# Two arms per expert, a 32-wide chunk for tokens 65 to 96, half-row scatters and branch hints in a mixture-of-experts kernel

## The chip, the cores and the metric

The kernel runs on 1 core of one Trainium2 chip. The metric is the device time of one execution in microseconds (us); the profile is one execution taken by the hardware profiler. TensorE is called PE here, VectorE DVE, ScalarE ACT, GpSimd POOL, and SyncE, whose queue issues the weight loads, SP.

## The reference

One encoder layer for 256 tokens of width 1024: three token mixers, gates, an output projection and a layer norm, and then a mixture of experts with a second layer norm. The mixers are not touched. The part that matters:

```python
logits = t @ router_w + router_b                    # 256 tokens, 32 experts
top_vals, top_idx = lax.top_k(logits, 4)
gates = softmax(top_vals)
# tokens are grouped by expert; for each expert e and its tokens xe:
h = xe @ w_gu[e] + b_gu[e]                          # 1024 -> 2 x 1024
gate, up = h[:, :1024], h[:, 1024:]
gate = minimum(gate, 7.0); up = clip(up, -7.0, 7.0)
y = ((up + 1) * (gate * sigmoid(1.702 * gate))) @ w_dn[e] + b_dn[e]
out[token] += y * gate_of(token, e)
x = layernorm(DN_ALPHA * x + out)
```

How many tokens an expert gets is known only on the chip.

## The kernel before

The first 396 us of the profiled execution are the mixers and the router; from there on the program walks through the 32 experts in order (`for e in range(NE)`), and ends with the second layer norm.

**Weights.** Expert e has 12 tiles of 1 MB: u0 to u7 for the gate-up product (one per 128 rows of the contraction) and u8 to u11 for the down product. `load(e, u)` puts them into a ring of 19 slots in that order, from SP's queue. A slot is free again when the last matmul that reads its tile has run, and tile u7 of the next expert takes the slot of u0 of this one (seven slots are free beyond an expert's twelve); 8 loads are in flight at most.

**Three arms.** The count of tokens is read from memory into registers of PE, ACT and DVE (`count`, L1294), and two compares choose the arm: L1337 (`rv > TINY`, 32) and inside it L1338 (`rv > CAP`, 64).
- `tiny` (up to 32 tokens): four matmuls at a time on four column groups of 32; tile names end in `t` (`pGU16t`, L1183; down product `pY16t`, L1203).
- `light` (33 to 64): pairs of 64 columns; tiles `pGU` (L1139, L1144) and `pY` (L1162).
- `heavy` (65 to 128): 128 columns; it gathers its own tokens (`heavy_gather`, tiles `pgx15h`, `pgt15h`) with a one-hot that `heavy_onehot` makes on DVE for every expert; gate-up `pGU15h` (L1239), down `pY15h` (L1265).

More than 128 tokens are handled ahead of the last expert, under a compare of its own (L1329). In the profiled run 19 experts take `tiny`, 10 `light` and 3 (experts 2, 15, 17) `heavy`.

**Inside an arm** PE's order is written by hand: bias matmul, gate-up over k = 0 to 7, with another expert's work after k = 1 (`fill` gathers or transposes the tokens of the next pair; `flush(prev)` scatters the expert before), the gates (`gate_slots`) after k = 5, the SwiGLU on DVE and ACT (`swiglu`), a second piece of other work, transposes (`pT`), down product. Then `weigh` splits y times gate into a high and a low part `yh` (ACT) and `yl` (DVE).

**The scatter.** `scatter_lhs` makes the 0/1 matrix `sc` that puts rows back to tokens, as two versions (two `is_equal`, L1112): the result rows of the two column halves stand in partitions 0 to 63 and 64 to 127, and each version has zeros for the other half. `flush` then runs 8 matmuls (L1123, L1124), each over 128 rows, and DVE adds the four results to the accumulator (L1126).

Of the kernel before, what the change touches and what calls it, by code (L numbers as in the profile page):

```python
# [18 lines left out]
P = 128  # L19
D = 1024  # L20
S = 256
# [8 lines left out]
TINY = 32  # L30
LIMIT = 7.0
# [109 lines left out]
def _consts():  # L141
# [26 lines left out]
    slot = np.full((P, 6), -5.0)  # L168
    slot[:64, 0] = p[:64] + 1
    slot[64:, 1] = p[:64] + 1  # L170
    slot[:, 2] = p + 1
    slot[:, 3] = p + 1 + P
    slot[:64, 4] = p[:64] % TINY + 1
    slot[64:, 5] = p[:64] % TINY + 1
# [8 lines left out]
def tile_trunk(ctx, tc, xT_d, xn_d, wf_d, vec_d, row_d, rw_d, cst_d, cst2_d, rope_d, ln1_d, ln2_d,  # L183
# [934 lines left out]
    def scatter(c, n, sc, ys, name):  # L1118
        po = sm(f"pos{name}{c}{n}")
        ls = sc[:, c * P:(c + 1) * P]  # L1120
        w = 512 // len(ys)
        for i, (yh, yl) in enumerate(ys):
            T.matmul(po[:, i * w:(i + 1) * w], ls, yh, start=True, stop=False)  # L1123
            T.matmul(po[:, i * w:(i + 1) * w], ls, yl, start=False, stop=True)  # L1124
        dst = acc[:, c, n * 512:(n + 1) * 512]
        V.tensor_add(dst, dst, po)  # L1126

    def flush(prev):
        if prev:
            e, sc, yh, yl = prev  # L1130
            for c in range(2):
                for n in range(2):
                    scatter(c, n, sc[:, n], [(yh, yl)], f"{e}")

    def light(e, oh, xg, bl, wt, prev, cur, fill):
# [18 lines left out]
        scatter_lhs(e, (0, 1), sc, f"{e}")  # L1154
# [11 lines left out]
    def tiny(e, oh, xg, bl, wt, prev, cur, fill):  # L1166


        nm = f"{e}t"
# [10 lines left out]
        lo = (e % 2) * CAP  # L1180
        for k in range(KT):
            for g, (h, q) in enumerate(quarters):
                T.matmul(grp(ps, g).rearrange("p (g n) -> p g n", g=2), xg[:, k, lo:lo + TINY],  # L1183
                         quarter(wt[k], h, q), start=False, stop=(k == KT - 1))
            if k == 1:
                fill("t") if e % 2 else flush(prev)
            if k == 5:
                gsl = gate_slots(lambda c: oh[:, c, e % 2, 0:TINY], e, nm)
# [5 lines left out]
        flush(prev) if e % 2 else fill("t")  # L1194
        scatter_lhs(e, (4, 5), sc, nm)
        hT = turned(uv, nm, bank(1, f"pT{nm}", [P, 2, P]))
        for b in range(2):
            for h in range(2):
                g = 2 * h + b
                last_ = (b, h) == (1, 1)  # L1200
                for j in range(2):
                    for n in range(2):
                        T.matmul(grp(pY, 2 * n + j), hT[:, j, g * TINY:(g + 1) * TINY],  # L1203
                                 wt[KT + 2 * b + h][:, j, n * 512:(n + 1) * 512],
                                 start=(j == 1 and (b, h) == (0, 0)), stop=last_)
        weigh(pY, gsl, yh, yl)

    def heavy_onehot(e, part):
        oh = ex.tile([P, 2, P], F32R, tag=("ohx", "sg")[part], name=f"ohx{e}h{part}", bufs=2)
# [292 lines left out]
```

## Time and profile before

| | us |
|---|---|
| median of 3 runs (lowest to highest) | 1447.0 (1443.74 to 1450.92) |
| the profiled execution, its own time | 1446.26 |
| its span, first to last instruction | 1444.4 |
| PE busy | 1139.7 (79%) |
| DVE busy | 622.1 (43%) |
| ACT busy | 322.8 (22%) |
| DMA queue 1 (data), share of 16 engines | 79.6%, 454.33 MB |
| DMA queue 8 (instructions) | 120 packets, 1.97 MB |

The averages mix stages with different limits. The stretch to read is the one from 412 us on, by stretches with their DMA rate, and in it the gaps on PE. An idle time whose releaser is called "issue" is one in which the engine waited for nothing that the profile shows.

### The profile page before, as it was taken

To read this page: it belongs to the slowest core of one execution; us is meant where nothing else is said; L and a number is where in the kernel's file an instruction comes from. 1 tells how busy PE (TensorE), PEld (TensorE's weight loads), DVE (VectorE), ACT (ScalarE), POOL (GpSimd) and SP (SyncE) were. 2 spreads that over 40 slices of the span, in tenths; PEclk is the share of its full clock that TensorE was granted. 3 is DMA by queue.
4 is the path that set the end of the run, shared out by engine and by line. 5 is a ranking of instruction groups with operands and counts; after the bars stand their busy time and mean duration, and the time that the engine had idled before them with its cause. 6 is when DMAs were issued, how large, how long until landed. Compare 5 with 4: busy or idle time off the path is not lost. (4 is left out here: it accounts for less than half of the span.)

```text
span 1444.4 us, 18035 instructions
## 1 busy us (share of the span) xinstructions
PE 1139.7 (79%) x6902; PEld 635.4 (44%) x6902; DVE 622.1 (43%) x1289; ACT 322.8 (22%) x651; POOL 294.1 (20%) x293
## 2 busy tenths in 40 slices
PE   8797696899965998778597859869978678766666
PEld 8686586899722442233132325334322233221223
DVE  5999996876642232224222323313232312232203
ACT  5465463654411111011010101111100101100001
POOL 5999999533120000000000000000000000000000
PEclk9998788999888999899798979979999989999778
DMA  7243333477869689999999999966999999999950
GB/s 248 100 146 117 113 133 108 159 237 271 334 234 415 262 341 413 415 415 413 415 415 416 414 413 409 363 260 262 416 413 415 415 415 415 414 414 416 415 231 29
DMA packets 89524, 456.79 MB, mean 316 GB/s; under 512 B 8304, under 2 KB 8704, under 8 KB 58496
## 3 DMA queue, kind: packets, MB, share of 16 engines
q1 hardware_dynamic: 89344, 454.33, 79.6%
q8 instruction: 120, 1.97, 0.6%
q14 instruction: 60, 0.49, 0.1%
HBM read 453.25 MB, written 1.05 MB: 315 GB/s over the span
## 5 line engine op out<-in xcount | busy, mean ns | idle before, releaser
L1391 POOL TENSOR_TENSOR xn<-xn,lb 128x256 f32<-128x256 f32 x4 | 2.8, 726 | 1027.1 <-DVE xn L1379 1027.1
L1144 PE MATMUL pGU<-ew,xg 128*64 128x512 f32 x640 | 159.4, 649 | 0.7 <-issue 0.7
L1126 DVE TENSOR_TENSOR xn<-xn,pos 128x512 f32<-128x512 f32 x124 | 77.1, 680 | 134.0 <-issue 116.1
L393 POOL TENSOR_TENSOR cbc<-cbc,ups 128x256 f32<-128x256 f32 x120 | 123.4, 1029 | 4.6
L248 DVE TENSOR_TENSOR wl<-raw,wh 128x1024 fp32r<-128x1024 f32 (+1 forms) x72 | 99.9, 1394 | 37.3 <-ACT wh L247 37.1
L247 ACT CAST wh<-raw 128x1024 fp32r<-128x1024 f32 (+1 forms) x89 | 91.0, 1030 | 57.0 <-DMA raw<-in_wf_dram 23.4
L392 POOL TENSOR_TENSOR ups<-ups,vec 128x256 f32<-128x256 f32 x120 | 102.2, 871 | 0.0
L1144 PEld LDWEIGHTS pGU<-ew,xg 128*64 128x64 f32 x640 | 46.7, 149 | 95.9 <-issue 94.2
L1162 PE MATMUL pY<-ew,hT 128*64 128x512 f32 x320 | 75.1, 624 | 0.0
L1139 PE MATMUL pGU<-bgu_t,bl 128*128 128x512 f32 x20 | 10.9, 643 | 75.4 <-issue 74.7
L1081 ACT ACTIVATE sg<-gv 128x256 f32<-128x256 f32 x20 | 8.3, 417 | 224.2 <-DVE gv L1079 224.2
L1123 PE MATMUL pos<-yh,sc 128*128 128x512 f32 x124 | 52.8, 426 | 1.7 <-DVE yl L1116 1.7
L248 POOL TENSOR_TENSOR wl<-raw,wh 128x1024 fp32r<-128x1024 f32 x17 | 42.2, 2488 | 52.1 <-ACT wh L247 40.5
L1124 PE MATMUL pos<-yl,sc 128*128 128x512 f32 x124 | 48.8, 394 | 0.0
L1162 PEld LDWEIGHTS pY<-ew,hT 128*64 128x64 f32 x320 | 23.1, 144 | 45.1 <-issue 44.4
L1116 DVE SCALAR_TENSOR_TENSOR yl<-pY,gsl,yh 128x512 fp32r<-128x512 f32 x10 | 7.5, 750 | 80.4 <-ACT yh L1115 80.4
L1139 PEld LDWEIGHTS pGU<-bgu_t,bl 128*128 128x128 f32 x20 | 4.6, 287 | 82.7 <-issue 82.7
L1123 PEld LDWEIGHTS pos<-yh,sc 128*128 128x128 f32 x124 | 23.3, 188 | 29.0 <-issue 21.9
L403 DVE SCALAR_TENSOR_TENSOR xacc<-xp,vec,xacc 128x256 f32<-128x256 f32 x48 | 35.6, 746 | 0.5
L1105 DVE COPY gsl<-pgs 128x1 f32<-128x1 f32 x10 | 1.6, 158 | 76.8 <-PE pgs L1103 76.8
L291 PE MATMUL px<-xh,wh 128*128 128x256 f32 x96 | 29.9, 312 | 5.9 <-ACT pt L553 4.8
L293 PE MATMUL px<-xh,wl 128*128 128x256 f32 x96 | 28.9, 301 | 0.4 <-DVE wl L248 0.4
(1235 smaller groups left out, 2567.4 us busy)
## 6 DMA issues: line engine op xcount, KB each, us to landing
ew<-in_wgu_dram SPq DMA_DIRECT2D x241, 1024.0 KB, 19.9
ew<-in_wdn_dram SPq DMA_DIRECT2D x124, 1024.0 KB, 19.4
raw<-in_wf_dram SPq DMA_DIRECT2D x87, 512.0 KB, 3.6
ew<-in_wgu_dram SPq DMA_DIRECT2D x30, 512.0 KB, 6.3
ew<-in_wdn_dram SPq DMA_DIRECT2D x8, 512.0 KB, 5.7
xraw<-in_xT_dram SPq DMA_DIRECT2D x4, 256.0 KB, 5.1
xn<-in_xn_dram SPq DMA_DIRECT2D x2, 512.0 KB, 6.7
lnt<-in_ln_dram SPq DMA_DIRECT2D x2, 512.0 KB, 10.1
```

Source lines behind the costliest of these rows:

```text
L247: A.copy(h[:, b], raw[:, b])
L248: (PO if u in LOW_POOL else V).tensor_sub(l[:, b], raw[:, b], h[:, b].bitcast(F32))
L291: T.matmul(ps, wh, mh(k), start=(k == 0), stop=False)
L293: T.matmul(ps, wl, mh(k), start=False, stop=(k == nk - 1))
L392: PO.tensor_tensor(pr, up[:, j:j + S], W("cw31", c * 31 + j).to_broadcast([P, S]), op=ALU.mult)
L393: PO.tensor_add(acc, acc, pr)
L403: V.scalar_tensor_tensor(acc, xp[:, j:j + S], W("cw5", t * 5 + j), acc, op0=ALU.mult, op1=ALU.add)
L1123: T.matmul(po[:, i * w:(i + 1) * w], ls, yh, start=True, stop=False)
L1124: T.matmul(po[:, i * w:(i + 1) * w], ls, yl, start=False, stop=True)
L1126: V.tensor_add(dst, dst, po)
L1144: T.matmul(ps[q][h * 64:(h + 1) * 64].rearrange("p (g n) -> p g n", g=2), xg[:, k, s_], quarter(wt[k], h, q), start=False, stop=(k == KT - 1))
L1162: T.matmul(pY[n * 64:(n + 1) * 64], lhs, wt[KT + 2 * b + h][:, j, n * 512:(n + 1) * 512], start=False, stop=(b == 1 and h == 1 and j == 1))
```

## The change

**Arms.** `small` (up to 32) and `light` (above 32) remain, under one compare with a label, `If(rv <= TINY, label=f"few{e}")`. An expert with more than 64 tokens takes `light` for its first 64 and then, under `If(rv > CAP)` inside the Else, `extra_chunk` for tokens 65 to 96: a one-hot of 32 columns, 32 gather matmuls into `pg15m` (L1219), eight copies, and then the body of `tiny` on the same 12 weight tiles, with `flush(cur)` after k = 1. More than 96 tokens go to the block ahead of the last expert. `heavy_onehot` is no longer made for each expert.

**Scatter.** One `sc` with the rows of both halves; each matmul takes 64 rows (partitions 0 to 63 for the first half of the columns, 64 to 127 for the second), and the two halves go to two banks alternately.

**Hints.** The count of expert e + 1 is loaded before expert e's compare, and each arm of e begins on PE with a hint for the branch `few{e+1}`, whose register is the value of `counts[e + 1] > TINY`.

```diff
-    def scatter_lhs(e, slots, sc, name):
+    def scatter_lhs(e, slot_, sc, name):
...
-        for i, s_ in enumerate(slots):
-            V.tensor_scalar(sc[:, i], pbr, C("slot", s_, s_ + 1), None, op0=ALU.is_equal)
+        V.tensor_scalar(sc, pbr, C("slot", slot_, slot_ + 1), None, op0=ALU.is_equal)
...
+    def scatter(pos, c, sc, ys, start=True):
+        for i, y in enumerate(ys):
+            for n in range(2):
+                r = slice(n * 64, (n + 1) * 64)
+                T.matmul(pos[n], sc[r, c * P:(c + 1) * P], y[r], start=(start and i == 0), stop=(i == 1))
...
+    def extra_chunk(e, bl, wt, cur):
+        nm = f"{e}m"
+        oh = ex.tile([P, 2, TINY], F32R, tag="ohm", name=f"oh{nm}", bufs=1)
+        for c in range(2):
+            V.tensor_scalar(oh[:, c], C("iota_s", 0, TINY), rank[c][:, e:e + 1], -float(CAP),
+                            op0=ALU.subtract, op1=ALU.is_equal)
+        pg = sm(f"pg{nm}", [P, KT, TINY])
+        for k in range(KT):
+            for c in range(2):
+                for i, src in enumerate((nh_, nl_)):
+                    T.matmul(pg[:, k], src[:, c, k * P:(k + 1) * P], oh[:, c],
+                             start=(c == 0 and i == 0), stop=(c == 1 and i == 1))
+        xg = ex.tile([P, KT, TINY], F32, tag="xge", name=f"xg{nm}", bufs=1)
+        for k in range(KT):
+            xcopy(xg[:, k], pg[:, k], k)
+        tiny(nm, e, lambda c: oh[:, c], xg, bl, wt, cur, 2, lambda: flush(cur), lambda: None)
...
+    def hint(e):
+        if e + 1 < NE:
+            tc.mark_branch_hint_location(f"few{e + 1}", hint=counts[e + 1] > TINY, engines=(ENG.PE,))
...
-            with tc.If(count(NE, ALL) > P):
+            with tc.If(count(NE, ALL) > TOP):
...
-        rv = count(e, (ENG.PE, ENG.Activation, ENG.DVE))
-        with tc.If(rv > TINY) as some:
-            with tc.If(rv > CAP) as cond:
-                heavy(e, 0, ohx, wt, prev, cur, fill)
-            with cond.Else():
+        rv = counts.pop(e)
+        if e + 1 < NE:
+            counts[e + 1] = count(e + 1, (ENG.PE, ENG.Activation, ENG.DVE))
+        with tc.If(rv <= TINY, label=f"few{e}") as few:
+            with tc.manual_schedule(engines={mybir.EngineType.PE}):
+                hint(e)
+                small(e, oh, xg, bl, wt, prev, cur, fill)
+        with few.Else():
+            with tc.manual_schedule(engines={mybir.EngineType.PE}):
+                hint(e)
+                light(e, oh, xg, bl, wt, prev, cur, fill)
+            with tc.If(rv > CAP):
                 with tc.manual_schedule(engines={mybir.EngineType.PE}):
-                    light(e, oh, xg, bl, wt, prev, cur, fill)
-        with some.Else():
-            with tc.manual_schedule(engines={mybir.EngineType.PE}):
-                tiny(e, oh, xg, bl, wt, prev, cur, fill)
+                    extra_chunk(e, bl, wt, cur)
```

The first place is PE at expert 15, where the code of `tiny` ends and that of `light` begins. Before:

```order
L1203 MATMUL pY15t<-ew_15_11_11853,hT15t 32x512 x4
L1337 UNCONDITIONAL_BRANCH
L1338 COMPARE_AND_BRANCH
L1139 MATMUL pGU_12083<-bgu_t,bl_11371 128x512
L1139 MATMUL pGU_12084<-bgu_t,bl_11371 128x512
L1144 MATMUL pGU_12083<-ew_15_0_11831,xg_10354 64x512 x2
```

Now, at the same place:

```order
L1197 MATMUL pY15t<-ew_15_11_10959,hT15t 32x512 x4
L1334 UNCONDITIONAL_BRANCH
L1291 REGISTER_ALU
L1495 BRANCH_PREFETCH_HINT
L1136 MATMUL pGU_11099<-bgu_t,bl_10535 128x512
L1136 MATMUL pGU_11100<-bgu_t,bl_10535 128x512
L1141 MATMUL pGU_11099<-ew_15_0_10937,xg_9640 64x512 x2
```

The second compare (L1338) stood between the two arms; it is gone from there, and a register operation and the hint stand in its place.

The second place is PE at the end of `light` of expert 15. Before, the code of `heavy` followed behind a jump:

```order
L1162 MATMUL pY_12144<-ew_15_10_11851,hT_1_12189 64x512 x4
L1162 MATMUL pY_12144<-ew_15_11_11853,hT_1_12189 64x512 x4
L1338 UNCONDITIONAL_BRANCH
L980 MATMUL pgt15h_11867<-cst,rawx 128x128 x4
L980 MATMUL pgt15h_11876<-cst,rawx 128x128 x4
```

Now the compare with 64 follows, and straight behind it the gather of the extra chunk:

```order
L1159 MATMUL pY_11160<-ew_15_10_10957,hT_1_11204 64x512 x4
L1159 MATMUL pY_11160<-ew_15_11_10959,hT_1_11204 64x512 x4
L1342 COMPARE_AND_BRANCH
L1219 MATMUL pg15m<-oh15m,nh 128x32
L1219 MATMUL pg15m<-oh15m,nl 128x32
```

The jump at the end of `light` has become a compare, and the extra chunk begins after the last down product of `light`.

The third place is `flush` in the light arm of expert 15, on PE. Before, each bank gets its two matmuls in a row:

```order
L1123 MATMUL pos_12162<-yh,sc 128x512
L1124 MATMUL pos_12162<-yl,sc 128x512
L1123 MATMUL pos_12166<-yh,sc 128x512
L1124 MATMUL pos_12166<-yl,sc 128x512
L1123 MATMUL pos_12170<-yh,sc 128x512
```

Now two banks take turns:

```order
L1117 MATMUL pos_11178<-yh,sc 128x512
L1117 MATMUL pos_11179<-yh,sc 128x512
L1117 MATMUL pos_11178<-yl,sc 128x512
L1117 MATMUL pos_11179<-yl,sc 128x512
L1117 MATMUL pos_11186<-yh,sc 128x512
```

The number of matmuls stays at eight; neighbours now work on different halves of the rows and write different banks.

## Rows read from the trace of the kernel before

**Rows 1.** Stretches: length; PE, PEld, DVE, ACT, POOL busy (count); PEclk, DMA share, GB/s

```profile
470.00:520.00 50.00, 49.65 (x145) 23.63 (x145) 13.95 (x33) 5.18 (x12) 0.00 (x0) 1.00 0.67 252
...
900.00:920.00 20.00, 20.00 (x75) 9.01 (x73) 6.45 (x17) 3.40 (x8) 0.00 (x0) 1.00 0.80 308
...
950.00:1010.00 60.00, 58.25 (x174) 29.75 (x174) 17.81 (x44) 8.70 (x21) 0.00 (x0) 0.94 0.61 231
1010.00:1370.00 360.00, 270.14 (x1737) 98.69 (x1737) 99.43 (x247) 34.46 (x74) 0.00 (x0) 0.90 1.02 415
```

**Rows 2.** DMA rate in 2-us slices, 440 to 520 us and 940 to 1020 us

```profile
GB/s 422 422 412 410 406 401 412 401 430 418 414 422 410 422 414 422 336 78 66 406 324 254 8 0 0 227 328 328 338 328 418 418 426 320 16 0 176 369 279 426
...
GB/s 426 397 422 414 418 422 418 385 86 0 0 0 33 295 371 344 14 137 387 264 289 352 418 250 49 348 332 311 12 0 33 311 229 414 414 414 430 408 393 412
```

**Rows 3.** SP's queue: what the weight loads waited for, 860 to 1012 us; issues; landing

```profile
SPq L732 <- PE pGU17h L1239: 30.4, 2, 24.4
...
859.66 18.43 SPq L732 DMA_DIRECT2D ew<-in_wgu_dram  x8
...
DMA to landing us min/median/max: 4.7/19.9/21.5
```

**Rows 4.** PE in order of time, arm beginnings: start, us, instructions, idle before and releaser

```profile
461.77 0.76 PE L966 MATMUL pgx2h<-nh,ohx2h 128*128 128x512 f32 x1 [14.99 <-issue]
...
864.46 1.97 PE L980 MATMUL pgt15h<-cst,rawx 128*128 128x128 f32 x8 [16.02 <-issue]
...
951.37 1.97 PE L980 MATMUL pgt17h<-cst,rawx 128*128 128x128 f32 x8 [14.82 <-issue]
...
1107.60 1.93 PE L1178 MATMUL pGU22t<-bgu_t,bl 128*32 128x512 f32 x8 [3.97 <-issue]
```

**Rows 5.** Instruction queue, packets and MB, in three gaps: before a small, light, heavy arm

```profile
q8 instruction: 1, 0.02, 1.1%
...
q8 instruction: 2, 0.03, 1.1%
...
q8 instruction: 3, 0.05, 1.3%
```

**Rows 6.** PE in order of time: end of 14, beginning of 16, light 18 whole

```profile
844.80 3.64 PE L1203 MATMUL pY14t<-ew,hT14t 128*32 128x512 f32 x32 [0.53 <-ACT hT14t L1094]
...
917.67 1.07 PE L1178 MATMUL pGU16t<-bgu_t,bl 128*32 128x512 f32 x8
918.56 1.90 PE L1183 MATMUL pGU16t<-ew,xg 128*32 128x512 f32 x16
...
1005.69 0.70 PE L1139 MATMUL pGU<-bgu_t,bl 128*128 128x512 f32 x2 [0.38 <-PE pos17h L1124]
...
1035.86 1.94 PE L1178 MATMUL pGU19t<-bgu_t,bl 128*32 128x512 f32 x8 [2.54 <-issue]
```

**Rows 7.** PE in order of time, pieces of small 22 and 23, first and last of eight scatters

```profile
1111.91 0.50 PE L1123 MATMUL pos<-yh,sc 128*128 128x512 f32 x1
...
1113.63 0.39 PE L1124 MATMUL pos<-yl,sc 128*128 128x512 f32 x1
...
1136.09 1.09 PE L980 MATMUL pgt23t<-cst,rawx 128*128 128x128 f32 x8
```

**Rows 8.** ACT and DVE in order of time: weighing, the two comparisons for the scatter

```profile
1381.62 0.69 ACT L1115 ACTIVATE yh<-pY,gsl 128x512 fp32r<-128x512 f32 x1 [9.32 <-PE pY L1162]
...
1415.00 0.86 DVE L1112 TENSOR_SCALAR sc<-pbr,cst 128x256 fp32r<-128x256 f32 x2
```

**Rows 9.** PE in order of time, the last two experts (30 and 31), and SP's last issues

```profile
1347.87 1.19 PE L1139 MATMUL pGU<-bgu_t,bl 128*128 128x512 f32 x2 [10.56 <-issue]
...
1397.98 1.19 PE L1139 MATMUL pGU<-bgu_t,bl 128*128 128x512 f32 x2 [12.67 <-issue]
...
1418.26 8.67 PE L1162 MATMUL pY<-ew,hT 128*64 128x512 f32 x32
...
1369.12 22.21 SPq L735 DMA_DIRECT2D ew<-in_wdn_dram  x4
```

More of the change, by code (lines that the diff above doesn't have):

```diff
@@ L30 @@
 TINY = 32
+TOP = CAP + TINY
 LIMIT = 7.0
@@ L1116, in weigh, with add @@
         V.scalar_tensor_tensor(yl, pY, gsl, yh.bitcast(F32), op0=ALU.mult, op1=ALU.subtract)
[L1118 to L1124, printed above, removed]
+    def scatter(pos, c, sc, ys, start=True):
[3 more added lines that the diff above has]
+                T.matmul(pos[n], sc[r, c * P:(c + 1) * P], y[r], start=(start and i == 0), stop=(i == 1))
+    def add(c, n, po):
         dst = acc[:, c, n * 512:(n + 1) * 512]
@@ L1260, in heavy @@
-        pY = [bank(n, f"pY{nm}{n}") for n in range(2)]
-        for n in range(2):
-            T.matmul(pY[n], bls[n], bdn_t, start=True, stop=False)
-        def down(n, b, h, j):
-            T.matmul(pY[n], hT[h, b][:, j], wt[KT + 2 * b + h][:, j, n * 512:(n + 1) * 512],
-                     start=False, stop=(b == 1 and h == 1 and j == 1))
-        for b in range(2):
-            for h in range(2):
-                for j in range(2):
-                    if (b, h) == (1, 1):
-                        continue
-                    for n in range(2):
-                        down(n, b, h, j)
@@ L1275, in heavy @@
[L1275 to L1287 removed]
+        scatter_lhs(e, 3 + part, sc, nm)
@@ new lines, in heavy @@
+        hT = {hq: turned(swiglu(ps[hq], f"{nm}_{hq[0]}{hq[1]}"), f"{nm}_{hq[0]}{hq[1]}") for hq in qs}
+        for n in range(2):
+            pY = bank(n, f"pY{nm}{n}")
+            T.matmul(pY, bls[n], bdn_t, start=True, stop=False)
+            for b in range(2):
+                for h in range(2):
+                    for j in range(2):
+                        T.matmul(pY, hT[h, b][:, j], wt[KT + 2 * b + h][:, j, n * 512:(n + 1) * 512],
+                                 start=False, stop=(b == 1 and h == 1 and j == 1))
+            weigh(pY, gsl, yh, yl)
+            for c in range(2):
+                po = sm(f"pos{nm}{c}{n}")
+                for i, y in enumerate((yh, yl)):
+                    T.matmul(po, sc[:, c * P:(c + 1) * P], y, start=(i == 0), stop=(i == 1))
+                add(c, n, po)
@@ L1359, in total, with add1 @@
                     T.matmul(pz[c][n], C("ident"), acc[:, c, n * 512:(n + 1) * 512], start=True, stop=False)
-            for n in range(2):
-                for i, y in enumerate((yh, yl)):
-                    T.matmul(pz[c][n], sc[:, n, c * P:(c + 1) * P], y, start=(c == 1 and i == 0), stop=(i == 1))
-        def add(n):
+            scatter(pz[c], c, sc, (yh, yl), start=(c == 1))
+        def add1(n):
             dst = acc[:, 1, n * 512:(n + 1) * 512]
```

97 lines of the change are left out of this document (34 added, 63 removed).

## The prediction

> **What bounds the kernel now.** I read the DMA rate by stretches first. From 1010 to 1370 us the queues move 415 GB/s [rows 1], which is their steady level in this kernel; a 1 MB tile then takes 2.53 us and an expert's twelve 30.3 us. So the weights set the pace, and PE's work costs time only where it keeps a ring slot so long that loads stop. The stretches where they stop are those around the three heavy experts: 252, 308 and 231 GB/s [rows 1]. Against 415 GB/s the lost time is 50 x (1 - 252/415) = 19.6 us at expert 2, 20 x (1 - 308/415) = 5.2 us behind expert 15 and 60 x (1 - 231/415) = 26.6 us behind expert 17; together 51.4 us. The view of SP's waits names the cause: loads wait up to 24.4 us for a heavy gate-up matmul [rows 3]. The slices show where the data ran dry: the rate falls at 473.6 us and at 956.4 us (336 and 86 GB/s as shares of a 2-us slice) [rows 2].
>
> Next come the gaps on PE. Its time between two arms is idle with the releaser "issue", and its length goes in steps: 3.97 us from a small arm to a small one [rows 4], 10.6 us from a small arm to a light one [rows 9], 15.0, 16.0 and 14.8 us from a small arm to a heavy one [rows 4]. In such gaps the instruction queue brings 1, 2 and 3 packets [rows 5]. One more compare that doesn't fall through is one more packet and about 5 to 6 us. At the end weights no longer bound: the last four loads are issued from 1369 to 1391 us, and PE stands 12.7 us before expert 31 and then works to the end [rows 9].
>
> **The change part by part.** All times are on the scale of the profiled execution, 1446.3 us, which lies 0.7 us below the median.
>
> *Entry of a heavy expert.* One compare of two goes, so the gap falls from 15.3 (mean of three) to a light arm's; with 10.6 and rows like it between 9.4 and 11.0 I take 10.3. Saved: 5.0 us of PE each.
>
> *Body of a heavy expert.* Before: 864.46 to 917.67, 53.2 us [rows 4, 6]. After: a light visit and the extra chunk. The light visit of expert 18 is 1005.69 to 1035.86 - 2.54 = 27.6 us [rows 6]. It loses one of two comparisons that take 0.86 us together [rows 8], 0.43, and part of the scatter: eight matmuls start 0.24 us apart, 1.9 us in all [rows 7]. That pairs on different halves of the rows run at once isn't shown here, but four column groups do (16 matmuls of a small arm in 1.90 us, 4 x 0.48) [rows 6]. I take half, 0.94, with 0 as the other end. So 27.6 - 1.4 = 26.3 us; experts 15 and 17 do transposes (1.1 us [rows 7]) where 18 does a gather of about 1.9, so 25.5.
>
> The extra chunk, until it has read the first weight tile: it waits for the weighing of the 64 tokens (0.69 on ACT [rows 8] and about as much on DVE) and two one-hots of below 0.43 each: 2.3. Then 32 gather matmuls; the nearest row is eight 128x128 transposes in 1.09, 0.136 each [rows 7]: 4.4. Copies that aren't hidden 0.5, bias 1.07, and the first of eight gate-up steps 0.93 [rows 6]. Sum 9.2 us, with 6 and 12 as ends (gathers twice as fast or as slow, copies in line or hidden). Behind it: seven gate-up steps 6.5, scatter 0.94, bias of the down product about 1.0, SwiGLU and transposes 2.4, down product 3.64 (as in a small arm [rows 6]): 14.5. The chunk is 23.7, the whole visit 50.0 (49.2 for 15 and 17): only 3 to 4 us shorter than before.
>
> *Which slot is late.* This matters more than the visit's length. Before, tiles were freed one by one over the visit. Now none is free until the extra chunk has read it, and then they come free every 0.93 us, faster than 2.53. So the first tile decides. From issue to landing takes at least 4.7 us [rows 3], 2.2 before the bytes flow.
> - Expert 2: the arm before ends at 461.77 - 14.99 = 446.8 [rows 4]. First slot at 446.8 + 10.3 + 26.3 + 9.2 = 492.6, bytes at 494.8; dry since 473.6. Loss 21.2 instead of 19.6: +1.6.
> - Expert 15: the arm before ends at 848.4 [rows 6]; first slot at 848.4 + 10.3 + 25.5 + 9.2 = 893.4, bytes at 895.6. Expert 16's u0 is issued at 859.7, lands 19.9 later, and u6 six tiles on, at 894.7 [rows 3]. Loss 0.9 instead of 5.2: -4.3.
> - Expert 17: expert 15 ends at 848.4 + 10.3 + 49.2 = 907.9; small 16 takes 951.37 - 14.82 - 917.67 = 18.9 [rows 4, 6], less 1.4, so 925.7 with the step between. First slot at 925.7 + 10.3 + 25.5 + 9.2 = 970.7, bytes at 972.9; dry at 956.4 - 4.3 = 952.1. Loss 20.8 instead of 26.6: -5.8.
> Sum of the heavies: -8.5 us. An error of x in the 9.2 counts at 2 once and at 17 twice: 3x.
>
> *Tail.* Expert 31's gap loses the second compare, -5.0; light 30 gets 1.4 shorter and its scatter 0.9; light 31 0.4; the last scatter 0.5, since only its first results are waited for. Sum -8.2 (-5 without the pairs).
>
> *What costs nothing.* Register loads and the hint lengthen each arm by some tenths at most, and a small visit with its gap is 22.9 us against 30.3 of loads; the cover is gone at 15 to 17 and at the end, where they are within the error. The one-hots taken off DVE hid in its idle time. Where small and light arms get shorter between 1010 and 1370 us, loads stay the bound.
>
> *The hint.* Nothing in this trace has one. From below: it does nothing, and gaps stay. From above: the gap before a light arm becomes that before a small one, 10.3 to 4.0. I take the lower end. The arm in which the hint stands goes on for 19 to 28 us and ends in a jump that itself brings a packet [rows 5]. And the register says `counts[e + 1] > TINY` while the branch is written `rv <= TINY`: by the gaps, small is the way that costs nothing, so a hint that speaks of the written condition speaks for the wrong way.
>
> [...]
>
> **Sum:** 1446.3 - 8.5 - 8.2 = 1429.6, say 1430 us. With 3 us either way in the extra chunk (9 us) and the scatter's 0, 1420 to 1441.
>
> **Rivals.**
> *The hint works.* Each heavy gap falls by another 6.3: expert 2 loses 14.9 (-6.3), 15 nothing (-0.9), and 17's first slot comes 12.6 earlier, with dry time 0.9 earlier (-11.7): -18.9. In the tail 30's gap gives 6.3 and 31's about 5, and PE stands less; the cap is the last tile: issued at about 1391, landed by some 8 us later, and read for 2 us, 1402 against PE's 1418.26 + 8.67 = 1426.9 [rows 9], so at most 25 us with the 8.2 in it; I take 24. Total 1446.3 - 8.5 - 18.9 - 24 = 1395 us (1388 to 1405). For it: the hint stands where the gap is made; against it: the two reasons above.
>
> *The hint speaks for the wrong way and throws out the next code.* Then a small arm pays about 5.3 us more. Alone, 22.9 + 5.3 = 28 is still under 30.3; it shows at expert 16, ahead of 17's first slot: +5.3, 1435 us.
>
> *The extra chunk comes later than thought, and the time ends above before.* Its code lies behind `light`'s and has its own compare on PE, ACT and DVE. Each packet that it must wait for is 5.3 us ahead of the first slot, and counts three times, 15.9. Break-even is 16.7 / 3 = 5.6 us per chunk: one packet gives 1446, two give 1462 us, since the twelve slots held are exactly what the loads then lack. For it: no run has executed code at this place, and 2.54 us are lost even behind light 18 [rows 6], where the old `light` jumped past `heavy`. Against: the arm that follows a compare directly costs no packet beyond the jump's own [rows 5].
>
> **How the numbers follow.** Chances: forecast 0.45 (1420 to 1441), hint works 0.31, wrong way 0.09, late chunk 0.15 (about half of it at one packet). The likeliest is 1430. The range runs from 1388 (the good end of the working hint) to 1444, which leaves out about 0.08 below and 0.1 above. 0.5% of 1447 is 7.2 us, about what a measurement of this kernel tells from no change: below 1439.8 lie nearly all of the first two and most of the third, 0.80; 0.11 lie within; 0.09 above.
>
> **What would show it.** Gaps on PE before light arms at 9.4 to 11 us mean that the hint does nothing, 4 or less that it works, and small arms with an inner gap of 5 that it harms. The loads' stop behind expert 2 should be as long as before and that behind 17 shorter by about 6; `pg15m` should follow `pY` by 2 to 3 us, and the first gate-up row of `pGU15m` by another 6. Expert 31's gap should be 7 to 8 us. The prediction is wrong in its core if the loads stop for another tile than the first, or if the end is set by something other than these waits.

## The result: 57 us slower

The changed kernel takes 1502.7 us (median of 4 runs, 1500.9 to 1503.9), the kernel before, run beside it, 1445.4 (1438.1 to 1450.9). The ratio is 1.040 with an interval of 1.035 to 1.045. The forecast was 1430 with a range up to 1444: wrong in sign and out of the range. The profiled execution took 1503.9 us, its span is 1502.0; before 1446.3 and 1444.4.

First the page: busy time of PE, and the instruction queue (packets, MB, share of the DMA engines). Of the kernel before:

```profile
PE 1139.7 (79%) x6902; PEld 635.4 (44%) x6902; DVE 622.1 (43%) x1289; ACT 322.8 (22%) x651; POOL 294.1 (20%) x293
...
q8 instruction: 120, 1.97, 0.6%
```

Of the changed kernel:

```profile
PE 1138.3 (76%) x7322; PEld 602.6 (40%) x7322; DVE 599.7 (40%) x1187; ACT 319.0 (21%) x636; POOL 291.9 (19%) x293
...
q8 instruction: 123, 2.02, 0.5%
```

PE is busy for as long as before, so the 57 us are time in which PE stands. The stretches of the changed kernel, with the columns of [rows 1], say where the loads stood:

```profile
470.00:500.00 30.00, 27.65 (x143) 12.76 (x141) 7.62 (x18) 2.85 (x6) 0.00 (x0) 0.96 0.16 67
500.00:540.00 40.00, 33.97 (x218) 12.52 (x220) 8.47 (x21) 4.79 (x11) 0.00 (x0) 0.86 0.77 316
540.00:560.00 20.00, 16.84 (x100) 5.97 (x100) 8.57 (x20) 2.29 (x5) 0.00 (x0) 1.00 0.29 106
560.00:900.00 340.00, 241.57 (x1481) 85.97 (x1475) 77.98 (x182) 31.72 (x67) 0.00 (x0) 0.86 1.00 405
920.00:945.00 25.00, 23.22 (x156) 11.32 (x153) 4.92 (x12) 2.21 (x5) 0.00 (x0) 0.80 0.60 234
995.00:1030.00 35.00, 31.84 (x204) 13.16 (x202) 10.72 (x26) 3.81 (x9) 0.00 (x0) 0.85 0.37 130
1050.00:1070.00 20.00, 17.55 (x94) 6.72 (x90) 5.07 (x13) 2.86 (x6) 0.00 (x0) 1.00 0.43 169
1070.00:1380.00 310.00, 210.31 (x1400) 71.70 (x1400) 70.56 (x163) 28.08 (x59) 0.00 (x0) 0.86 1.00 407
1430.00:1502.00 72.00, 44.52 (x196) 19.25 (x192) 17.27 (x42) 5.77 (x11) 2.77 (x4) 0.78 0.37 141
```

Reckoned as in the prediction (length times 1 - rate/415), the first two lines are the stop at expert 2: 25.2 + 9.5 = 34.7 us, where [rows 1] had 19.6. The third is a stop that the kernel before did not have, behind light 3: 14.9. Behind expert 15 10.9 are lost instead of 5.2. At 17 and behind light 18 it is 24.0 + 11.9 instead of 26.6. Where the loads ran at 415 before, from 520 to 900 and from 1010 to 1370, they now run at 405 (8.2 lost, from 560 to 900) and at 407 (6.0 lost). From 412 to 470 us they run at 386 instead of 406 (4.1 lost instead of 1.3). Together some 115 us of loading are lost up to 1430 us, where the kernel before lost 53; the difference of 62 is the 57 us to within 5. The end costs nearly what it cost before: 72 x (1 - 141/415) = 47.5 us in the last line, and in the last 74 us of the kernel before, at 139 GB/s, 49.2. So the stops at 2 and 15 grew, new ones came behind light arms, and none got shorter but 17's own.

What the weight loads waited for, in SP's queue from 412 to 1480 us (total, times, longest):

```profile
SPq L727 <- PEq L1342: 164.9, 9, 32.7
...
SPq L727 <- PE pGU2m L1178: 46.7, 3, 45.8
...
SPq L727 <- PE pGU17m L1178: 37.6, 3, 36.7
```

Line 1342 is `with tc.If(rv > CAP)`, the compare of the extra chunk, and PEq is PE's sequencer. Nine times a load waited for that compare, so not for a matmul. Before, a light arm freed its tiles one by one: from 412 to 1400 us the loads waited for a matmul of line 1144, a light arm's gate-up, 9.2 us at the longest.

```profile
SPq L732 <- PE pGU L1144: 36.5, 13, 9.2
```

PE's own waits in the changed kernel, from 412 to 1480 us: the gaps ahead of light arms and then every stop of over 3 us inside an arm:

```profile
PE pGU L1136 <- issue: 107.8, 12, 11.4
PE pGU21t L1178 <- issue: 6.8, 1, 6.8
PE pGU5t L1178 <- issue: 6.7, 1, 6.7
PE pGU23t L1178 <- issue: 6.7, 1, 6.7
...
PE pGU9t L1178 <- issue: 6.2, 1, 6.2
PE pGU27t L1178 <- issue: 6.0, 1, 6.0
...
PE pGU1t L1178 <- issue: 5.6, 1, 5.6
...
PE pGU29t L1178 <- issue: 5.5, 1, 5.5
...
PE pGU13t L1178 <- issue: 4.0, 1, 4.0
...
PE pGU19t L1178 <- issue: 3.9, 1, 3.9
...
PE pGU11t L1178 <- issue: 3.5, 1, 3.5
```

Line 1136 is the first matmul of a light arm (as 1139 in the kernel before), so its 107.8 us are the gaps ahead of lights. Line 1178 is a gate-up matmul in the middle of an arm. Ten small arms stand still there, every one of an odd expert, 54.9 us in all. PE in order of time shows the first of them and what it does to expert 2 (start, length, instructions, idle before and releaser); in the last line small 4, behind light 3, waits 1.78 us for DVE to pass the compare on line 1342:

```profile
427.86 1.93 PE L1174 MATMUL pGU1t<-bgu_t,bl 128*32 128x512 f32 x8 [4.35 <-issue]
429.54 3.66 PE L1178 MATMUL pGU1t<-ew,xg 128*32 128x512 f32 x14
438.81 1.86 PE L1178 MATMUL pGU1t<-ew,xg 128*32 128x512 f32 x2 [5.60 <-issue]
...
465.18 1.19 PE L1136 MATMUL pGU<-bgu_t,bl 128*128 128x512 f32 x2 [9.51 <-issue]
466.30 5.78 PE L1141 MATMUL pGU<-ew,xg 128*64 128x512 f32 x16
472.01 0.50 PE L1117 MATMUL pos<-yh,sc 64*128 64x512 f32 x2
472.35 0.39 PE L1117 MATMUL pos<-yl,sc 64*128 64x512 f32 x2
...
487.36 7.09 PE L1159 MATMUL pY<-ew,hT 128*64 128x512 f32 x32
496.32 0.25 PE L1219 MATMUL pg2m<-oh2m,nh 128*128 128x32 f32 x1 [1.87 <-DVE oh2m L1213]
...
501.77 1.94 PE L1174 MATMUL pGU2m<-bgu_t,bl 128*32 128x512 f32 x8
503.48 2.53 PE L1178 MATMUL pGU2m<-ew,xg2m 128*32 128x512 f32 x16
...
554.90 1.06 PE L1174 MATMUL pGU4t<-bgu_t,bl 128*32 128x512 f32 x8 [1.78 <-DVEq L1342]
```

In the kernel before the same small arm began at 428.71 and the gap ahead of expert 2 at 446.8, so it took 18.1 us. Now it runs from 427.86 to 465.18 - 9.51 = 455.67, which is 27.8. The stop itself is 5.60; the rest is slower matmuls on both sides of it: the changed kernel needs 3.66 us for the 14 gate-up matmuls ahead of the stop where the one before did 16 in 2.52, and behind it the transposes, 1.09 us at a granted clock of 1.00 [rows 7], took 1.97 at 0.50. PE's granted clock is 0.51 from 427 to 433.2 us, behind the gap ahead of the arm. It has risen to 1.00 when the stop begins (433.2 to 436), falls while PE stands and is 0.50 from 436.5 to 442; in the kernel before it is 0.76 from 430.4 to 433 and 1.00 from 434 to 438. PE's records show no branch between 427.5 and 438.8 us, so the stop is not a jump.

### The profile page after: what moved, and what is told of

It reads as the page before. It is cut to its first block, busy times and chain, and to the rows that moved or that the text cites. A ratio compares the mean times of both kernels' runs of the same rounds, so it can differ in the third digit from the quotient of the medians.

```text
span 1502.0 us, 18859 instructions
## 1 busy us (share of the span) xinstructions
PE 1138.3 (76%) x7322; PEld 602.6 (40%) x7322; DVE 599.7 (40%) x1187; ACT 319.0 (21%) x636; POOL 291.9 (19%) x293
## 5 line engine op out<-in xcount | busy, mean ns | idle before, releaser
L1141 PE MATMUL pGU<-ew,xg 128*64 128x512 f32 x832 | 212.1, 659 | 1.1 <-issue 1.1
L1121 DVE TENSOR_TENSOR xn<-xn,pos 128x512 f32<-128x512 f32 x136 | 84.6, 681 | 141.5 <-PE pos L1117 141.5
L388 POOL TENSOR_TENSOR cbc<-cbc,ups 128x256 f32<-128x256 f32 x120 | 121.4, 1012 | 4.6
L1141 PEld LDWEIGHTS pGU<-ew,xg 128*64 128x64 f32 x832 | 64.3, 152 | 127.4 <-issue 123.0
L1136 PE MATMUL pGU<-bgu_t,bl 128*128 128x512 f32 x26 | 15.0, 678 | 107.8 <-issue 107.8
L1159 PE MATMUL pY<-ew,hT 128*64 128x512 f32 x416 | 95.3, 612 | 0.0
L1159 PEld LDWEIGHTS pY<-ew,hT 128*64 128x64 f32 x416 | 29.6, 141 | 56.6 <-issue 55.9
L1117 PE MATMUL pos<-yh,sc 64*128 64x512 f32 x136 | 30.5, 444 | 1.8 <-DVEq L1342 1.8
L287 PE MATMUL px<-xl,wh 128*128 128x256 f32 x96 | 28.7, 299 | 0.0
L1109 ACT ACTIVATE yh<-pY,gsl 128x512 fp32r<-128x512 f32 x13 | 8.9, 687 | 90.2 <-PEq L1342 68.7
```

Of the source, the lines that this page charges most:

```text
L287: T.matmul(ps, wh, ml(k), start=False, stop=False)
L388: PO.tensor_add(acc, acc, pr)
L1117: T.matmul(pos[n], sc[r, c * P:(c + 1) * P], y[r], start=(start and i == 0), stop=(i == 1))
L1141: T.matmul(ps[q][h * 64:(h + 1) * 64].rearrange("p (g n) -> p g n", g=2), xg[:, k, s_], quarter(wt[k], h, q), start=False, stop=(k == KT - 1))
L1159: T.matmul(pY[n * 64:(n + 1) * 64], lhs, wt[KT + 2 * b + h][:, j, n * 512:(n + 1) * 512], start=False, stop=(b == 1 and h == 1 and j == 1))
```

## The experiments

Fifteen kernels were run. Times are medians of four runs or more with the ratio to the kernel before in the same batch (95% interval); one is a single run, and says so. "Small first" means that the small arm's code lies directly behind the expert's compare, as in both kernels.

### The hints

**e1_no_hint**: the changed kernel without the two calls.

```diff
-                hint(e)
                 small(e, oh, xg, bl, wt, prev, cur, fill)
...
-                hint(e)
                 light(e, oh, xg, bl, wt, prev, cur, fill)
```

> The changed kernel without the hints; all else stays. Theory A (the hint's fetch goes ahead of the next block of the running arm, so small arms whose code crosses a block early stand still): the inner gaps of 3.5 to 6.8 us in ten odd small arms (54 us together) go away, visits of odd small arms fall from about 28 to 19 us, and the time falls to 1430 to 1450 us. Theory B (the gaps come from the new layout of the code, the hint does nothing): inner gaps and time stay, 1495 to 1510 us. Theory C (the extra chunk's held tiles are the cost): time falls by under 10 us.

Measured: 1478.7 us, 1.026 (1.023 to 1.029). The hints cost some 20 to 24 us of the 57 (1.4% by the two ratios, 24 us by the medians). In PE's waits only 2.9 us at small 20 and 1.4 at 22 are left for "issue" at line 1178. So theory A was right on the inner gaps, but the time stayed 29 us above its 1430 to 1450: the hints are not the whole loss. Without them expert 2 begins at 453.27 us instead of 465.18, and 26.5 us of loading are lost there (452 to 512 us at 232 GB/s) instead of 34.7.

**e2_flip**: the same calls with the other sign.

```diff
-            tc.mark_branch_hint_location(f"few{e + 1}", hint=counts[e + 1] > TINY, engines=(ENG.PE,))
+            tc.mark_branch_hint_location(f"few{e + 1}", hint=counts[e + 1] <= TINY, engines=(ENG.PE,))
```

> The changed kernel with the hint's condition turned round (count of the next expert <= 32). If the value decides what is fetched: gaps ahead of light arms fall from 9.5 us to 4 or less. If the value doesn't matter: gaps of 9.3 to 11.4 us ahead of light arms, the same ten odd small arms with inner gaps, and 1495 to 1510 us.

Measured: 1460.3 us in a single run, 13 us below the lowest of e1's four. The stops inside small arms fall from 54.9 to 1.7 us (1.4 at expert 5 and 0.3 at 23), with the same instructions at the same places. So it is the sign of the hint that makes them. The gaps ahead of lights stay at 9.5 to 11.5 where a small arm was before: even the other sign does not shorten them, so neither expectation held whole. From light to light, ahead of experts 7 and 25, they are 2.1 and 2.1, where the changed kernel has 7.0 and 7.0 and e1 1.8 and 5.5.

**e4_before_hint**: the kernel before, with the counts read one expert ahead and the hints as the change has them.

```diff
+            tc.mark_branch_hint_location(f"few{e + 1}", hint=counts[e + 1] > TINY, engines=(ENG.PE,))
...
+                    hint(e)
...
+                hint(e)
```

> The kernel before with the hints alone (early counts, label and hint in the small and light arms). Theory A: small arms get inner gaps of 3 to 7 us, 1465 to 1500 us. Theory B (layout): no new gaps, 1440 to 1452 us.

Measured: 1466.1 us, 1.016 (1.013 to 1.019): 23 us slower, with nothing of the change but the hints and the early counts, which this run does not separate. Here other arms are hit (entry of 11 7.4 us instead of none, inside 20 6.7, 27 6.2, 13 5.0), so what is hit changes with the code and does not belong to the expert.

### The block behind light

**e3_three**: no hints, and no block behind light: light, or a second copy of light with the extra chunk in the same arm (edit against e1).

```diff
-            with tc.manual_schedule(engines={mybir.EngineType.PE}):
-                light(e, oh, xg, bl, wt, prev, cur, fill)
-            with tc.If(rv > CAP):
+            with tc.If(rv <= CAP) as one:
                 with tc.manual_schedule(engines={mybir.EngineType.PE}):
+                    light(e, oh, xg, bl, wt, prev, cur, fill)
+            with one.Else():
+                with tc.manual_schedule(engines={mybir.EngineType.PE}):
+                    light(e, oh, xg, bl, wt, prev, cur, fill)
                     extra_chunk(e, bl, wt, cur)
```

> No hints, and three arms: small, light, and a copy of light with the extra chunk behind it, so that light has no compare behind its down product. Theory (light's inner compare makes PE wait for DVE's last step behind each light arm): the 1.78 us waits for DVE ahead of ten arms go away, and the time is 3 to 12 us below that of the run without hints. Rival (those waits are hidden under the loads): within 3 us of it, or above by up to 15 us since a heavy expert pays two compares again.

Measured: 1453.6 us, 1.008 (1.005 to 1.011). Against e1 the block costs 25 us, more than the 3 to 12 expected: the theory was about a wait of 1.78 us for DVE, and what went away is the hold on the tiles. In e1 SP's queue still has the wait that the changed kernel has (line 1340 is there the same compare); in e3 there is none:

```profile
SPq L727 <- PEq L1340: 150.7, 9, 32.2
```

The stop of the loads goes with it. Light 3 begins at 510 us in e1 and at 511 in e3; the stretch from there on, first e1 (14.6 us lost) and then e3 (nothing lost):

```profile
512.00:552.00 40.00, 36.08 (x227) 13.32 (x225) 12.64 (x30) 4.50 (x10) 0.00 (x0) 1.00 0.66 264
```

```profile
512.00:552.00 40.00, 36.16 (x188) 12.39 (x190) 11.14 (x26) 3.93 (x9) 0.00 (x0) 0.90 1.02 414
```

**e5_hold** and **e6_join**: does the block cost because it reads the weights, or because of the join? The kernel before gets an If behind light that is never taken (no count exceeds 200 here). In e5 its body reads all twelve tiles; in e6 it reads the identity instead.

```diff
+                with tc.If(rv > 200):
+                    with tc.manual_schedule(engines={mybir.EngineType.PE}):
+                        pd = sm(f"pd{e}", [P, P])
+                        for u in range(12):
+                            w_ = wt[u] if u < KT else wt[u][:, 0]
+                            T.matmul(pd, w_[:, 0:P], C("ident"), start=(u == 0), stop=(u == 11))
```

and for e6, against e5:

```diff
-                            w_ = wt[u] if u < KT else wt[u][:, 0]
-                            T.matmul(pd, w_[:, 0:P], C("ident"), start=(u == 0), stop=(u == 11))
+                            T.matmul(pd, C("ident"), C("ident"), start=(u == 0), stop=(u == 11))
```

> The kernel before, with one thing added behind light: an If that is never taken here (count over 200) whose body reads all twelve weight tiles of the expert. Theory (a block behind light that may read the tiles holds all twelve slots of every light expert until PE has passed its compare): SP's loads wait for that compare up to 30 us at a time, the data rate falls behind light experts, and the time rises by 10 to 30 us. Rival (only the wait of the engines for each other at the join costs): as the next run.

> The same If behind light, never taken, whose body reads no weight tile. Theory of the held slots: tiles are freed one by one as before, only the join is left, 0 to 8 us above the kernel before. Rival (the join is the cost): as much as the run in which the body reads the tiles.

Measured: e5 1435.0 us, 0.994 (0.991 to 0.997); e6 1418.9, 0.983 (0.980 to 0.986). Reading the tiles in a block that never runs costs 16 us, the difference of the two. In e5 SP waits 20.3 us at the longest for that compare, in e6 2.8 (3.5 us in all):

```profile
SPq L732 <- PEq L1343: 25.3, 2, 20.3
```

But against the kernel before both came out the other way than expected: e5 is 8 us faster instead of 10 to 30 slower, and e6, which only adds work that is never done, is 25 us faster. The reason stood in the gaps, of both runs: in e6 ahead of lights behind small arms -0.1 instead of 9 to 11 us, from light to small 9.3 to 9.7 instead of -0.1. These are the gaps of an order in which small lies last, as the next run has it.

### The order of the arms

**e9_small_last**: the kernel before with one argument more.

```diff
-        with tc.If(rv > TINY) as some:
+        with tc.If(rv > TINY, preferred_fallthrough_block=True) as some:
```

> The kernel before with one word changed: the branch on 32 tokens is laid out with the small arm last, so that a small arm runs on into the next expert's compares and light or heavy follow those without a jump; no block behind light. Theory (which arm lies next to the next compare decides where the gaps fall; the run with the block that reads nothing was faster for that alone): gaps ahead of light and heavy arms behind small ones fall from 9 to 16 us to below 1, gaps ahead of small arms behind light ones rise from 0 to about 9, and the time is 1408 to 1425 us. Rival (the speed of that run came from the join itself): 1440 to 1450 us.

Measured: 1414.3 us, 0.979 (0.976 to 0.982). The instructions of the arms are the same. PE's waits of the kernel before, from 412 to 1400 us, and then those of e9:

```profile
PE pGU L1139 <- issue: 74.7, 8, 12.7
```

```profile
PE pGU L1139 <- issue: 14.7, 3, 9.8
PE pGU13t L1178 <- issue: 11.4, 1, 11.4
...
PE pGU4t L1178 <- issue: 9.7, 1, 9.7
PE pGU8t L1178 <- issue: 9.6, 1, 9.6
```

The gaps ahead of lights fall from 74.7 to 14.7 us, those ahead of heavies from 15 and 16 [rows 4] to 2.5 and below, and light to small rises from about zero to between 9 and 11. The sum of the gaps is not the gain; their place is. A gap ahead of a small arm is covered by the loads, one ahead of a heavy arm is time in which no slot comes free, and one ahead of light 30 or 31 stands at the end of the program. From 412 to 1360 us the loads run at 400 GB/s instead of 392, 948 x 8/415 = 18 us; the gap ahead of light 30 falls from 10.56 [rows 9] to -0.1, that ahead of 31 from 12.67 to 9.8.

**e11_after_small_last**: the changed kernel, hints and block and all, with small last.

```diff
-        with tc.If(rv <= TINY, label=f"few{e}") as few:
+        with tc.If(rv <= TINY, label=f"few{e}", preferred_fallthrough_block=False) as few:
```

> The changed kernel, hints and all, with the small arm laid out last; the hint's register is then set when the branch is not taken. Theory (value 0 speaks for the jump: it now speaks the right way, and the layout saves the gaps ahead of light): no inner gaps in small arms, gaps ahead of light arms behind small ones near 0, the loads still stop behind light arms (held slots): 1435 to 1465 us. Rival (hints cost whatever they say): 1470 us or more.

Measured: 1430.1 us, 0.989 (0.986 to 0.992), 5 us below the range expected. This one argument moves the changed kernel by 73 us, from 4.0% slower to 1.1% faster. It does two things at once, since with the order of the arms it turns what the hint speaks for: here the hints as written help, small to small is -0.2 to 1.9 us instead of 4.2 to 6.0. The block still holds the slots (PEq L1342: 104.7 us in 9 waits, longest 33.0).

### The extra chunk, and putting it together

**e12_extra_last**: e3 (light, light with the chunk, small; no hints) with small last. **e13_interleaved_last**: the same, but the third arm takes each weight tile for the 64 tokens and for the 32 two steps later. **e7_interleaved** is that arm in e3's order. The core of the interleaved arm:

```diff
+        for k in range(KT):
+            mt(k)
+            if k + 2 < KT:
+                lt(k + 2)
```

> The layout of the small-last run (light, then the arm above 64, then small), no hints, no block behind light, half-row scatters; above 64 tokens light and behind it the extra chunk on the held tiles. Beside the small-last run, whose arm above 64 is the old heavy, it shows the chunk alone. Theory (the first slot comes late): loads stop 15 to 22 us at expert 2 and at 17, against 10 and 5, and the time is 10 to 20 us above the small-last run, 1424 to 1434. Rival (the chunk is as good as heavy): within 5 us of it.

> The same layout, with the interleaved arm above 64 tokens lying behind light, so that its exit passes the small arm alone. Theory (the 13.5 us gaps behind the interleaved arm in the earlier run came from a jump over two arms): they fall below 2 us, and the time falls from 1431 to 1400 to 1415 us. Rival (the interleaved arm itself is slow): 1425 us or more.

> Three arms without hints; in the third, tokens 65 to 96 are done together with the first 64: each gate-up tile is read by the extra chunk two steps behind the 64 tokens and then free, and the extra down product follows the first one. If the late first slot was the cost at the heavy experts: loss at expert 2 falls from 23 to about 10 us, at 15 and 17 from 30 to 10 or 15, and the time is 15 to 30 us below the three-arm run, 1425 to 1440. If the length of PE's visit was the cost: within 8 us of it.

Measured: e12 1412.2 us, 0.976 (0.972 to 0.981). It differs from e9 in the form of the heavies (and the scatter in halves) and lies within its interval: two chunks of 64 and 32 are worth as much as the old heavy arm, and the 10 to 20 us expected for a late first slot did not come. Against e3, which has its three arms with small first, e12 shows what the order is worth without hints: 1.008 to 0.976, 3.2%. e13 1403.8, 0.972 (0.968 to 0.976): freeing tiles from the start of the arm gives some 8 us, though the two intervals overlap. e7 1445.9, 1.002 (1.000 to 1.004): in the old order the same gives 8 us against e3 as well, where 15 to 30 were expected, and no more than brings it back to the kernel before.

**e10_best**: the interleaved arm (`wide`), but in the order wide, light, small (edit against e13).

```diff
-            with tc.If(rv <= CAP, preferred_fallthrough_block=True) as one:
+            with tc.If(rv > CAP) as one:
...
-                    light(e, oh, xg, bl, wt, prev, cur, fill)
+                    wide(e, oh, xg, bl, wt, prev, cur, fill)
...
```

> Small arm last, the interleaved arm for tokens 65 to 96 in place of heavy, half-row scatters, no hints, no block behind light. If the two gains add: the gaps of the small-last run and a loss of loads at the heavy experts below it, 1395 to 1415 us. If the interleaved arm gives nothing beside the layout: within 5 us of the small-last run.

Measured: 1431.4 us, 0.989 (0.985 to 0.993), 28 us behind e13 and 16 us above the range expected. Now the wide arm jumps over two others, and what follows it waits 13.5 us (experts 3, 16 and 18). In e13 that gap is 0.8 us at 3 and 6.6 at 18, but still 13.3 at 16, where a small arm follows. And light no longer lies next to the compare: from small to light the gap is 3.9 to 5.8 us, in e13 -0.1.

**e14_hints_right**: e13 with the hints as the change writes them, which in this order are right.

```diff
+                    hint(e)
                     light(e, oh, xg, bl, wt, prev, cur, fill)
...
+                hint(e)
                 small(e, oh, xg, bl, wt, prev, cur, fill)
```

> The run before with the hints as the change writes them, which is the right way round in this layout (0 speaks for the jump to the small arm). If right hints help: gaps from small to small fall from 4 to below 1 us and from light to small below 9, time 0 to 10 us lower. If they cost: inner gaps in small arms and 5 us or more above.

Measured: 1393.1 us, 0.965 (0.962 to 0.969): 51 us faster than the kernel before and 110 faster than the changed one. PE in order of time at the beginning of small 1, e13 and then e14:

```profile
430.62 1.93 PE L1174 MATMUL pGU1t<-bgu_t,bl 128*32 128x512 f32 x8 [4.38 <-issue]
432.30 3.67 PE L1178 MATMUL pGU1t<-ew,xg 128*32 128x512 f32 x16
```

```profile
425.80 1.04 PE L1174 MATMUL pGU1t<-bgu_t,bl 128*32 128x512 f32 x8
426.66 1.90 PE L1178 MATMUL pGU1t<-ew,xg 128*32 128x512 f32 x16
```

The gap is gone, and the matmuls behind it take half the time (1.90 instead of 3.67): the granted clock is 1.00 from 425.9 to 428.5 us in e14, and 0.50 in e13 from 430.6 to 434, behind its gap. PE's sequencer has a record for each branch, and the one ahead of small 1 says where the gap comes from, first e13 and then e14 (length in ns three times, start):

```profile
L1419 PEldq COMPARE_BRANCH  x1: 6532/6532/6532, 423.9 to 423.9; - x1
```

```profile
L1419 PEldq COMPARE_BRANCH  x1: 370/370/370, 423.7 to 423.7; - x1
```

It starts while the last matmuls of small 0 still run; so of the 6.53 us only 4.38 show as a gap. From light to small, where the light arm ends in a jump over two arms, the gap only falls from 9.3 to 7.8 us (experts 8 and 19), and ahead of light 31, at the end, it grows from 7.1 to 12.1. The instruction queue fetched 123 packets in e13 and here:

```profile
q8 instruction: 104, 1.70, 0.5%
```

### Do the costs add up?

**e15_three_hint** and **e8_three_flip**: e3 with the hints as written in all three arms, and with the other sign.

```diff
+                hint(e)
                 small(e, oh, xg, bl, wt, prev, cur, fill)
...
```

> The three-arm kernel (small first, no block behind light) with the hints as the change writes them: the change less the block behind light. If the two costs add (24 us for the hints, 25 for the block): about 24 us above the three-arm run without hints, 1475 to 1482, and 20 to 28 below the change. If the hints' harm needs the late loads that the block makes: within 12 us of the three-arm run, 1453 to 1466.

> The three-arm kernel with the hints, their condition turned round (count of the next expert <= 32). If a right hint shortens the gap ahead of light arms behind small ones: 11 us falls to 4 to 6, time 8 to 15 us below the three-arm run. If such a hint is lost at the jump that ends a small arm and only the harm of the wrong one is gone: gaps of 11 us stay, no inner gaps, time within 5 us of the three-arm run.

Measured: e15 1501.0 us, 1.040 (1.035 to 1.046); e8 1469.5, 1.018 (1.015 to 1.022). All expectations for the two missed. Taking the block away from the changed kernel gives nothing while the hints are in (1501 against 1503), though it gives 25 us once they are out; and the hints cost 47 us without the block, 20 to 24 with it. The costs don't add. With three arms both signs harm: in e8 the gaps ahead of third arms grow from e3's 11.3 to 13.2 us to as much as 18.8,

```profile
880.79 1.21 PE L1136 MATMUL pGU<-bgu_t,bl 128*128 128x512 f32 x2 [18.83 <-issue]
```

and e15 fetches 149 packets where e3 fetches 137. Why the hints cost twice as much there is not settled. On the one path that can be read off in steps, the 4.0% are 0.8 for chunk and scatter, with the code of a third arm, in this order of the arms (e3), 1.8 for the block (e1 over e3) and 1.4 for the hints (the changed kernel over e1).

## Why the prediction was wrong, step by step

*What bounds the kernel.* Right: the loads, and the gaps on PE only where they keep a slot. The rate of the loads from 412 to 1360 us and the time go together:

| kernel | GB/s | time, us |
|---|---|---|
| the change | 365 | 1502.7 |
| e1_no_hint | 375 | 1478.7 |
| e3_three | 388 | 1453.6 |
| before | 392 | 1445 |
| e5_hold | 394 | 1435.0 |
| e9_small_last | 400 | 1414.3 |
| e13_interleaved_last | 401 | 1403.8 |
| e14_hints_right | 405 | 1393.1 |

The other kernels fall in with this order to within 2 GB/s, but for e11, with its stops behind lights (389 and 1430.1).

*"Which slot is late" failed, since it was asked of three visits only.* The prediction says "Now none is free until the extra chunk has read it", and reckons this for experts 2, 15 and 17. But the extra chunk's block lies behind every light arm, taken or not, and what releases a slot is then PE's passing of the compare on line 1342. Each light visit so holds twelve slots to its end. The prediction named this as a sign of being wrong in its core: loads that stop for another tile than the first. The sum has no term for it; "What costs nothing" counted light arms as shorter by 1.4 us, under the cover of the loads. Measured: stops of 14.9 us behind light 3 and 11.9 behind light 18, the nine waits at line 1342, 16 us for such a block that only stands there (e5 against e6), and 25 in this kernel without hints (e1 against e3), where the stop behind light 3 goes with the block.

*"The hint" was mis-chosen and mis-sized.* The paragraph on the hint had the right reason, that it speaks for the wrong way, but took the value "nothing". The rival built on it had the sign and the mark ("small arms with an inner gap of 5": they are 3.5 to 6.8), a chance of 0.09 and a cost of 5 us in all; that the hint throws out code, as its name says, no run shows. Three sizes in it were off. The hit arm 1 pays 9.7 us, not 5.3: 5.60 are the stop, and the matmuls on both sides of it run at a granted clock of 0.51 and 0.50; against the same arms of the kernel before 5 pays 9.9, 9 8.7, and 11, 13 and 19, which follow a light arm, 4.8 to 7.5. With 22.9 us a small visit and its gap go to 22.9 + 9.7 = 32.6, above the 30.3 of the loads that were to cover it. And it does not show "at expert 16" alone, which is not even hit: it shows at expert 1, directly ahead of 2, which begins at 465.18 instead of the 446.8 + 10.3 = 457.1 of the sum. Measured: 20 to 24 us here, 23 on the kernel before.

*Expert 2 worked through.* Forecast of the first slot 492.6 us, loss 21.2. Measured: the first two gate-up steps of the chunk start at 503.48 and take 2.53, so the first is done at about 504.7; loss 34.7. Of the 12 us 8.1 come from the late start, 3.0 from a light visit of 29.3 us instead of 26.3 (its first 16 gate-up matmuls take 5.78 us at a granted clock of 0.62; the 16 of light 3 in the kernel before take 3.65 at 1.00), and 1.0 from the chunk's entry (10.3 instead of 9.2: the gather takes 501.77 - 496.32 = 5.5, forecast 4.4). Another 1.4 us of the loss I can't assign. The stop behind 15 is 10.9 instead of 0.9: gap 11.4 (forecast 10.3), light visit 28.9 (25.5) and entry of the chunk 11.5 (9.2) make 6.8 of the 10. The one at 17 is 24.0 instead of 20.8.

*"Tail" was mis-sized.* From the end of small 29 to the end of the span the kernel before takes 107.1 us and the changed one 104.5: 2.6 gained, forecast 8.2. The gap ahead of 31 gives 3.0 (forecast 5.0), the gap ahead of 30 1.1, and light 30 with its scatter 3.3 (forecast 2.3). But light 31 is 2.7 us longer, with a stop of 1.13 us for "issue" in its gate-up, and what follows its down product 2.0: PE's last matmuls wait 1.78 us for DVE to pass the compare on line 1342, where the kernel before went straight on.

*What was right.* The gaps ahead of the heavies fall from 15 to between 9.5 and 11.4 (forecast 10.3). The chunk takes 24.9, 26.5 and 26.6 us from the end of the 64 tokens (forecast 23.7). The scatter's pairs do run at once: an entry of two (472.01 and 472.35 above) takes 0.50 and 0.39 us, what a single one takes in [rows 7], and the eight end 1.2 us after the first begins, against 2.1 before. The rival of a late chunk can be laid aside: it follows pY by 1.8 to 1.9 us, and the compare behind the 64 tokens brings no gap of its own. Expert 31's gap is 9.71 us, forecast 7 to 8, before 12.67 [rows 9]:

```profile
1406.99 1.19 PE L1136 MATMUL pGU<-bgu_t,bl 128*128 128x512 f32 x2 [9.45 <-issue]
...
1450.86 1.19 PE L1136 MATMUL pGU<-bgu_t,bl 128*128 128x512 f32 x2 [9.71 <-issue]
```

*What the forecast gains were worth.* The chunk and the scatter without hints and block (e3) still lose 0.8% in this order of the arms, and nothing in the other (e12 against e9). So -8.5 us at the heavies was not there to be had by shortening the visit; e13 got 8 by freeing tiles earlier. What makes e3 slower than before, gaps behind its third arm or its code's length, was not separated.

*Jumps and packets.* Without hints the gap from small to small, in which the prediction found one packet, is there in either order of the arms: 3.9 to 5.8 us in e1, 3.9 to 4.8 in e9 (10.3 at expert 1). With right hints (e14) it is -0.2 at small 1, and the instruction queue brings 19 packets fewer than in e13 (104 instead of 123). What the hint does in between, no trace shows. PE's branch records go with the gaps: ahead of expert 2 the kernel before has three of over 5 us in a row (6.05, 5.39 and 5.57) and the changed one two (6.14 and 5.28), while a branch that goes straight on lasts about 0.1 (ahead of small 1 0.08 in the kernel before and 0.11 in the changed one).

What a hint for the wrong way does inside an arm stays open. The rows show that only odd small arms are hit in this kernel, others in e4, odd and even ones in e15 (7.5 us at 20, 6.1 at 26), and hardly any with the sign turned (e2, 1.7 us in all).

## What to carry to other kernels

A conditional block that reads a ring's tiles, put behind an arm, held the ring until that arm's compare even where it was never taken (loads waited for that compare up to 20.3 us in e5, 2.8 in e6, whose block reads no tile); put the block inside an arm of its own, so that the common arm frees its tiles one by one. Before shortening gaps, look at which arm lies next to the compare: the order of the arms is one argument in the code and was worth 2.1% on the kernel before and 3.2% between e3 and e12 (4.8% on the changed kernel, where it also set the hints right), as it moved gaps from where nothing covers them to where loads do. Turn the sign of a branch hint and run both: the stops inside small arms were 54.9 us with one sign (the changed kernel) and 1.7 with the other (e2), and here the same sign was wrong in one order of the arms and right in the other (e11).

## What the runs showed of the hardware

- A gap on PE of 4.4 us ahead of small 1 cost more than 4.4: the 16 matmuls that follow its bias took 3.67 us at a granted clock of 0.50 (e13), and 1.90 at 1.00 without the gap (e14). Small 1 with a stop of 5.6 us in it took 9.7 us longer (27.8 instead of 18.1, the changed kernel against the one before).
- A branch on PE that goes straight on lasted 0.08 and 0.11 us ahead of small 1 (before and changed), one in the gaps ahead of small 1 and of expert 2 5.3 to 6.5 (before, changed, e13); with a right hint the one ahead of small 1 took 0.37 (e14).
- Right hints took away the gap from small to small (4.4 to -0.2 us at small 1, e13 to e14), but only part of the one from light to small, behind an arm which itself ends in a jump (9.3 to 7.8 at experts 8 and 19, 16.7 to 10.4 at 11).
- Wrong hints did not bring more packets in the changed kernel: it and e1 both fetch 123 (e15 149 where e3 fetches 137). They made ten small arms stand 3.5 to 6.8 us in their middle.
- What an arm's end costs depended on the order of the arms: from light to small -0.1 us where small lies first (before; 2.5 at expert 19) and 9.1 to 11.4 where it lies last (e9), and 13.5 behind the wide arm that jumps over two others (e10).
